# Down matrices of a SwiGLU layer: the running product read by ScalarE copies, and B22's casts placed between two of them

## The chip, the cores and the metric

One core of one Trainium2 chip. The metric is the device time of one execution in microseconds (us), the median of several runs. The engines of the core are TensorE (PE in the profile; PEld is its weight load), VectorE (DVE), ScalarE (ACT), GpSimd (POOL) and SyncE (SP), whose queue issues the DMA transfers (SPq).

## The reference

One layer of a streaming-encoder trunk on x of 1024 tokens by 1024 features, all in float32: RMSNorm, a combined input projection, three groups of heads (spatial gating, a conformer convolution, a gated delta rule), an output projection and a residual; then the part of this study, a SwiGLU feed-forward with D_FF = 2816 and its residual, and a final RMSNorm.

```python
x = x + jnp.einsum("bte,ed->btd", mix, w_out[l])
h = rms_norm(x, ffn_norm_g[l])
ff = jax.nn.silu(jnp.einsum("btd,df->btf", h, w_gate[l])) * jnp.einsum("btd,df->btf", h, w_up[l])
x = x + jnp.einsum("btf,fd->btd", ff, w_down[l])
return rms_norm(x, final_norm_g)
```

## The kernel before

Activations stand transposed: features on the 128 partitions, tokens on the free axis, in two halves of 512. To keep float32 accuracy, each operand is split into a high part (a cast to fp32r on ScalarE) and a low part (original minus high part, on VectorE), and each product is made in three passes: high by high, high by low, low by high. `split` and `split_w` (L127 to 132) do the splitting.

The feed-forward matrices are multiplied block-wise in 2 by 2 blocks with 7 products instead of 8. A `Matrix` stands for one such set of weights; its seven weight blocks are named w1 to w7 and meet the seven activation blocks B11 (w1), B21 (w2), T2 (w6), T1 (w5), T3 (w7), T4 (w4) and B22 (w3). One product (`product`, L799 to 803) is 12 matmuls of 128x128 by 128x512: four slices of the contraction by three passes. The products w1, w6, w7 and w4 run on in one PSUM tile X: after each, the value of X is read out before the next product adds to it. w2 goes to Y, w5 and w3 to Z. GpSimd forms the sums s1, s2 and s3 of the weight blocks (L836 to 838), from which w6, w5 and w7 are split, and then s2 again (L847) for w3; this last sum overwrites s2 and so waits for w6's low part.

The list `seq` holds 22 gate and up matrices, then 8 down matrices in two groups of four: d00, d02, d04, d06 and d10, d12, d14, d16 (group, first output tile). A group covers 8 of the 22 tiles of the feed-forward's features; the last six are multiplied after the down matrices, into the tiles pdl. Each down matrix takes the activation blocks of its group, which the gate and up matrices left in DRAM (FFd). `Group.load` and `Group.split` (L1044 to 1067) fetch and split them; B22 and T3 keep their halves in wider tiles, named B22B22f and T3hT3f/T3lT3f in the profile. The residual xad of one output tile and token half is loaded (`acc`), added to by `add` (L1005 to 1009), and stored again (`put`, L1003) after its last addition.

A gate or up matrix copies X to SBUF on ScalarE after w1, w6 and w7 (c11, c12 and c22: L828, L863, L868), and VectorE works on the copy. A down matrix instead reads X on VectorE: `add` takes X, Y or Z from PSUM and adds it to the residual, seven times per matrix (from X four times, from Y once, from Z twice). The next product into X cannot start before the addition that reads X is done.

The main loop (L1119 to 1172) writes the program in this order for each matrix: product6, product5, product7, then w1 and w2 of the next matrix (`first`) where that is not done yet, the splits of the next matrix's other weights (`rest`), and w4 and w3 (`end`). Ahead of a group, the first two products of its second and third matrix are done early (`early`), and then those of its first. The order of each engine's instructions is settled by a scheduler from this program when the kernel is built; engines run their rows in order and wait on one another by semaphores. In the kernel before, the group's splits of T3, T4 and B22 stand at the end of the step of the last matrix ahead of the group. Weights come in raw tiles of 512 KB (`load_raw`, L136, two buffers) and are released when their last block is split or summed.

## Time and profile before

| | us |
|---|---|
| median of 3 runs (1170.41 to 1175.22) | 1175.08 |
| profiled execution | 1176.49 |
| its span in the profile | 1174.5 |
| TensorE busy | 1139.2 (97%) |
| VectorE busy | 794.1 (68%) |
| ScalarE busy | 482.1 (41%) |
| GpSimd busy | 300.9 (26%) |
| mean granted clock of TensorE | 0.989 of full speed |

The span runs from the first to the last instruction that the profiler recorded; the execution's own time has some 2 us around it. The busy time of TensorE is modelled from pipelined matmuls: one is recorded at 0.39 to 0.40 us, while the next starts 0.23 us later. The down matrices lie between 914 and 1098 us of the span. The chain of work that ended last is 82% TensorE, 6% VectorE, 5% DMA, 3% issue, 2% GpSimd and 1% ScalarE.

### The profile page before, as it was taken

Reading aid. Unit: us, or ns where it says so; the run is one execution under the profiler, and the core shown is the slowest. Engines: PE = TensorE matmul, PEld = TensorE weight load, DVE = VectorE, ACT = ScalarE, POOL = GpSimd, SP = SyncE. Lnnn points to the kernel's source line nnn. Section 1 sums busy time; section 2 is a strip of 40 time slices with the busy share of each in tenths; the row PEclk is TensorE's granted clock in tenths of the full one; section 3 lists DMA queues with packets and bytes.
Section 4 is the critical chain, followed back from the end, with each engine's and each line's share of the span. In section 5 each row is a group of like instructions: output and inputs, shape, how many; then the busy total and the mean of one; then the engine's idle time right before and its main releaser. Section 6 shows DMA issues by size and latency. Waiting matters only on the chain.

```text
span 1174.5 us, 16043 instructions
## 1 busy us (share of the span) xinstructions
PE 1139.2 (97%) x5878; PEld 940.2 (80%) x5878; DVE 794.1 (68%) x1250; ACT 482.1 (41%) x1007; POOL 300.9 (26%) x234
## 2 busy tenths in 40 slices
PE   9999999999899999979999999999999979989997
PEld 7889888889688778858888888888888867868897
DVE  7699879868987666686555655565445767856523
ACT  6456561224235644354333333333334523423422
POOL 3000140010613221244323333333332232232142
PEclk9999999999999999999999999999999989999998
DMA  6235342463313455314222322232335778678212
GB/s 222 69 94 185 109 126 108 117 206 112 123 65 108 134 180 170 109 54 151 100 99 90 126 90 99 90 126 90 107 126 175 247 258 278 213 252 293 93 63 82
DMA packets 87182, 162.66 MB, mean 138 GB/s; under 512 B 16416, under 2 KB 28352, under 8 KB 87104
## 3 DMA queue, kind: packets, MB, share of 16 engines
q1 hardware_dynamic: 87104, 161.64, 41.4%
q8 instruction: 46, 0.75, 0.3%
q14 instruction: 32, 0.26, 0.1%
HBM read 114.93 MB, written 46.68 MB: 138 GB/s over the span
## 4 chain that ended last, share of the span: by engine, by line
PE 82%; DVE 6%; DMA 5%; issue 3%; POOL 2%; ACT 1%; SPq 0%; POOLq 0%; DVEq 0%; ACTq 0%
PE Xu L802 10%; PE Xg L802 10%; PE po L727 7%; PE pdl L1087 5%; PE Xd L802 5%; PE Zu L802 5%; PE Zg L802 5%; PE pv L228 4%; PE pq L228 4%; PE pk L228 3%; PE Yu L802 3%; PE pg L228 2%; PE Yg L802 2%; PE Zd L802 2%; DMA d_r<-in_wd_dram 2%
## 5 line engine op out<-in xcount | busy, mean ns | idle before, releaser
L664 DVE SCALAR_TENSOR_TENSOR ca<-cy,vec,ca 128x512 f32<-128x512 f32 x120 | 93.6, 801 | 0.5
L836 POOL TENSOR_TENSOR s1u<-u_r 128x512 f32<-128x512 f32 x11 | 23.6, 2149 | 81.3 <-DMA u_r<-in_wu_dram 81.3
L131 DVE TENSOR_TENSOR wo_l<-wo_r,wo_h 128x512 fp32r<-128x512 f32 x32 | 27.0, 854 | 24.3 <-ACT wo_h L130 24.2
L836 POOL TENSOR_TENSOR s1d<-d_r 128x512 f32<-128x512 f32 x8 | 10.7, 1334 | 110.8 <-DMA d_r<-in_wd_dram 110.8
L869 DVE TENSOR_TENSOR c22u<-Zu,c22u 128x512 f32<-128x512 f32 x11 | 7.6, 692 | 45.3 <-ACT c22u L868 45.3
L847 POOL TENSOR_TENSOR s2g<-g_r,s2g 128x512 f32<-128x512 f32 x11 | 19.0, 1727 | 71.5 <-DVE w6g_l L131 63.4
L789 POOL TENSOR_TENSOR sqa<-sqa,xr 128x512 f32<-128x512 f32 x13 | 18.0, 1384 | 71.8 <-ACT xr L787 44.1
L1007 DVE TENSOR_TENSOR xad<-Xd,xad 128x512 f32<-128x512 f32 x32 | 21.9, 686 | 20.7 <-PE Xd L802 20.6
L1241 POOL TENSOR_TENSOR sqf<-sqf,sqt 128x256 f32<-128x256 f32 (+1 forms) x19 | 17.9, 941 | 69.6 <-ACT sqt L1239 67.9
L847 POOL TENSOR_TENSOR s2u<-u_r,s2u 128x512 f32<-128x512 f32 x11 | 18.5, 1679 | 59.9 <-DVE w6u_l L131 59.9
L836 POOL TENSOR_TENSOR s1g<-g_r 128x512 f32<-128x512 f32 x11 | 15.0, 1368 | 66.6 <-DMA g_r<-in_wg_dram 66.6
L130 ACT CAST wo_h<-wo_r 128x512 fp32r<-128x512 f32 x32 | 19.6, 616 | 28.2 <-PE po L727 19.9
L1087 PE MATMUL pdl<-ff_h,wd_h 128*128 128x256 f32 (+1 forms) x96 | 30.9, 322 | 0.0
L1087 PE MATMUL pdl<-ff_h,wd_l 128*128 128x256 f32 (+1 forms) x96 | 30.5, 318 | 0.0
L1087 PE MATMUL pdl<-ff_l,wd_h 128*128 128x256 f32 (+1 forms) x96 | 30.5, 318 | 0.0
L1232 DVE TENSOR_TENSOR xf<-pdl,xf 128x256 f32<-128x256 f32 (+1 forms) x18 | 9.2, 514 | 28.3 <-PE pdl L1087 28.3
L802 PE MATMUL Xg<-b,w1g_h 128*128 128x512 f32 x88 | 27.6, 394 | 0.0
L802 PE MATMUL Yu<-b,w2u_h 128*128 128x512 f32 x88 | 27.6, 394 | 0.0
L802 PE MATMUL Xu<-b,w1u_h 128*128 128x512 f32 x88 | 27.6, 394 | 0.0
L802 PE MATMUL Yg<-b,w2g_h 128*128 128x512 f32 x88 | 27.5, 394 | 0.0
L868 ACT COPY c22g<-Xg 128x512 f32<-128x512 f32 x11 | 6.5, 587 | 48.3 <-PE Xg L802 48.3
L727 PE MATMUL po<-myc_l,wo_h 128*128 128x512 f32 x64 | 25.6, 400 | 0.7 <-DVE myc_l L90 0.7
(580 smaller groups left out, 3927.9 us busy)
## 6 DMA issues: line engine op xcount, KB each, us to landing
u_r<-in_wu_dram SPq DMA_DIRECT2D x24, 512.0 KB, 3.9
d_r<-in_wd_dram SPq DMA_DIRECT2D x24, 512.0 KB, 4.2
g_r<-in_wg_dram SPq DMA_DIRECT2D x23, 512.0 KB, 3.7
wo_r<-in_wout_dram SPq DMA_DIRECT2D x16, 512.0 KB, 3.8
xad<-X1d SPq DMA_DIRECT2D x32, 256.0 KB, 4.4
X1d<-xad SPq DMA_DIRECT2D x28, 256.0 KB, 3.2
FFd<-T SPq DMA_DIRECT2D x24, 256.0 KB, 2.0
xr<-in_xT_dram SPq DMA_DIRECT2D x16, 256.0 KB, 3.6
```

Source lines behind the costliest of these rows:

```text
L130: ACT.copy(hi, raw)
L131: DVE.tensor_tensor(lo, raw, f32(hi), op=ALU.subtract)
L228: proj.last = PE.matmul(ps[hf], lhsT=cols(wtile, a, kt * P), rhs=(xh, xl)[b][kt][hf], start=(kt == 0 and a + b == 0), stop=(kt == KT - 1 a ...
L664: DVE.scalar_tensor_tensor(o, y(m), w(m), o, op0=ALU.mult, op1=ALU.add)
L727: out_mm.last = PE.matmul(ps, lhsT=cols(wtile, a, kt * P), rhs=mix[hf][kt][b], start=(kt == 0 and a + b == 0), stop=(kt == 3 and a == 1))
L789: POOL.tensor_tensor(acc, acc, xr, op=ALU.add)
L802: PE.matmul(ps, lhsT=w[a][:, k * P:(k + 1) * P], rhs=blk[b][k], start=(first and k == 0 and a + b == 0), stop=(last and k == HB - 1 and a ...
L836: POOL.tensor_tensor(self.s1, a21, a22, op=ALU.add)
L847: (eng or POOL).tensor_tensor(self.s2, self.part(0, 1), self.s2, op=ALU.subtract)
L1007: DVE.tensor_tensor(x, ps, x, op=ALU.add)
L1087: PE.matmul(ps[:, 0:cs.stop - cs.start], lhsT=cols(wtile, a, c), rhs=ff[f, hf][b][:, cs], start=(first and i + a + b == 0), stop=(last and ...
L1241: POOL.tensor_tensor(acc[:, 0:w], acc[:, 0:w], t[:, 0:w], op=ALU.add)
```

## The change

The three methods of a down matrix that multiply into X now call those of `Matrix`. ScalarE copies X to c11, c12 or c22; VectorE adds Y to c11 and Z to c22, and then the copy to the residual. The number of VectorE operations per matrix stays at seven: of the four that read X and the three that read Y or Z, one from X and one from Z stay additions from PSUM into the residual, two read PSUM into c11 or c22, and three have both inputs in SBUF. ScalarE gets three copies of 128x512 per down matrix, 24 in all. The casts and subtractions that split B22 move from the end of the step before the group to behind product6 of the group's first matrix.

```diff
@@ -1002,32 +1002,28 @@
             if self is not seq[-1]:
                 nc.sync.dma_start(X1d[self.f[i], hf], self.x[i, hf])
 
-        def add(self, i, hf, ps, last=False):
+        def add(self, i, hf, t, last=False):
             x = self.x[i, hf]
-            DVE.tensor_tensor(x, ps, x, op=ALU.add)
+            DVE.tensor_tensor(x, t, x, op=ALU.add)
             if last:
                 self.put(i, hf)
 
         def begin(self, mid=None):
-            n, self.x = self.name, {}
-            self.X, Y = mm_ps(f"X{n}"), aux(f"Y{n}")
+            self.x = {}
             self.acc(0, 0)
-            product(self.X, self.w1, self.blk["B11"], True, False)
-            self.add(0, 0, self.X)
-            product(Y, self.w2, self.blk["B21"], True, True)
-            self.add(0, 0, Y, True)
+            super().begin(mid)
+            self.add(0, 0, self.c11, True)
 
         def product6(self):
             self.acc(0, 1)
-            product(self.X, self.w6, self.blk["T2"], False, False)
-            self.add(0, 1, self.X)
+            super().product6()
+            self.add(0, 1, self.c12)
 
         def product7(self):
             for i in range(2):
                 self.acc(1, 1 - i)
-            product(self.X, self.w7, self.blk["T3"], False, False)
-            self.add(1, 1, self.X)
-            self.add(1, 1, self.Z, True)
+            super().product7()
+            self.add(1, 1, self.c22, True)
 
         def end(self):
             product(self.X, self.w4, self.blk["T4"], False, True)
@@ -1127,6 +1123,8 @@
             last_tiles()
         if i > 0:
             m.product6()
+            if i in opener:
+                opener[i].split("B22")
             if new:
                 new.split("B11")
             m.product5()
@@ -1166,7 +1164,6 @@
             new.split("T3")
             new.load("B22")
             new.split("T4")
-            new.split("B22")
         if i >= FT and nxt is not None and i + 4 >= len(seq):
             for k in (0, 1) if i + 4 == len(seq) else (2, 3) if i + 3 == len(seq) else (4, 5):
                 load_late(LAST + k, 0)
```

The methods of `Matrix` that are now called stand unchanged:

```python
        def begin(self, mid=None):
            n = self.name
            self.X, Y = mm_ps(f"X{n}"), aux(f"Y{n}")
            product(self.X, self.w1, self.blk["B11"], True, False)
            if mid:
                mid()
            self.c11 = dt(f"c11{n}")
            ACT.copy(self.c11, self.X)
            product(Y, self.w2, self.blk["B21"], True, True)
            DVE.tensor_tensor(self.c11, Y, self.c11, op=ALU.add)
...
        def product6(self):
            product(self.X, self.w6, self.blk["T2"], False, False)
            self.c12 = dt(f"c12{self.name}")
            ACT.copy(self.c12, self.X)

        def product7(self):
            product(self.X, self.w7, self.blk["T3"], False, False)
            self.c22 = dt(f"c22{self.name}")
            ACT.copy(self.c22, self.X)
            DVE.tensor_tensor(self.c22, self.Z, self.c22, op=ALU.add)
```

How this moves instructions, at three places. The names carry the matrix (w6d00_l is the low part of w6 of d00) and a buffer number; c, X, Y and Z are the tiles above.

ScalarE at the first down matrix. Before, around the first cast of B22:

```order
L130 CAST w4d00_h_8261<-d001_r_8169 128x512
L130 CAST w3d00_h_8266<-s2d00_8244 128x512
L1066 CAST B22B22f000_8311<-B22B22f010_8313 128x512
L130 CAST w6d02_h_8396<-s2d02_8391 128x512
L130 CAST w5d02_h_8400<-s1d02_8390 128x512
L1066 CAST B22B22f000_8311<-B22B22f010_8313 128x512
L1066 CAST B22B22f001_8312<-B22B22f011_8314 128x512 x2
L130 CAST w7d02_h_8404<-s3d02_8392 128x512
```

Now:

```order
L1062 CAST T4f0h3_8328<-T4f0l3_8018 128x512
L863 COPY c12d00_8351<-Xd00_8185 128x512
L1062 CAST B22B22f000_8317<-B22B22f010_8319 128x512 x2
L1062 CAST B22B22f001_8318<-B22B22f011_8320 128x512 x2
L868 COPY c22d00_8391<-Xd00_8185 128x512
L130 CAST w6d02_h_8406<-s2d02_8401 128x512
```

The four casts stood among those of d02's weights, and now stand between the copies of c12 and c22 of d00. In the second group, one of the four stands ahead of c12 of d10 and three behind it.

TensorE at the end of w7 of d00. Before:

```order
L802 MATMUL Xd00_8179<-T3lT3f01_8238,w7d00_h_8257 128x512
L802 MATMUL Xd00_8179<-T3hT3f01_8235,w7d00_l_8258 128x512
L802 MATMUL Xd02_8093<-T2f0h0_8210,w6d02_h_8396 128x512
L802 MATMUL Xd02_8093<-T2f0l0_7704,w6d02_h_8396 128x512
L802 MATMUL Xd02_8093<-T2f0h0_8210,w6d02_l_8397 128x512
L802 MATMUL Xd02_8093<-T2f0h1_8213,w6d02_h_8396 128x512
L802 MATMUL Xd00_8179<-T4f0h0_8319,w4d00_h_8261 128x512
```

Now:

```order
L802 MATMUL Xd00_8185<-T3lT3f01_8244,w7d00_h_8263 128x512
L802 MATMUL Xd00_8185<-T3hT3f01_8241,w7d00_l_8264 128x512
L802 MATMUL Xd00_8185<-T4f0h0_8325,w4d00_h_8267 128x512
L802 MATMUL Xd00_8185<-T4f0l0_8015,w4d00_h_8267 128x512
L802 MATMUL Xd00_8185<-T4f0h0_8325,w4d00_l_8268 128x512
```

Four matmuls of the next matrix's w6 stood between w7 and w4 of one matrix; now w4 follows w7 at once.

VectorE ahead of w6's low part of d00. Before, from w2's low part on:

```order
L131 TENSOR_TENSOR w2d00_l_8176<-d001_r_8169,w2d00_h_8175 128x512
L1067 TENSOR_TENSOR T1f0l0_7712<-T1f0l0_7712,T1f0h0_8222 128x512
L1007 TENSOR_TENSOR xad0400_8138<-Yd04_8137,xad0400_8138 128x512
L1067 TENSOR_TENSOR T1f0l1_7713<-T1f0l1_7713,T1f0h1_8225 128x512
L1067 TENSOR_TENSOR T1f0l2_7714<-T1f0l2_7714,T1f0h2_8228 128x512
L1067 TENSOR_TENSOR T1f0l3_7715<-T1f0l3_7715,T1f0h3_8231 128x512
L131 TENSOR_TENSOR w6d00_l_8250<-s2d00_8244,w6d00_h_8249 128x512
```

Now the last twelve of the sixteen that run from w2's low part to w6's:

```order
L1063 TENSOR_TENSOR T2f0l1_7705<-T2f0l1_7705,T2f0h1_8219 128x512
L1063 TENSOR_TENSOR T2f0l2_7706<-T2f0l2_7706,T2f0h2_8222 128x512
L830 TENSOR_TENSOR c11d00_8199<-Yd00_8186,c11d00_8199 128x512
L1063 TENSOR_TENSOR T2f0l3_7707<-T2f0l3_7707,T2f0h3_8225 128x512
L1007 TENSOR_TENSOR xad0000_8183<-c11d00_8199,xad0000_8183 128x512
L1063 TENSOR_TENSOR T1f0l0_7712<-T1f0l0_7712,T1f0h0_8228 128x512
L1063 TENSOR_TENSOR T1f0l1_7713<-T1f0l1_7713,T1f0h1_8231 128x512
L1063 TENSOR_TENSOR T1f0l2_7714<-T1f0l2_7714,T1f0h2_8234 128x512
L1063 TENSOR_TENSOR T1f0l3_7715<-T1f0l3_7715,T1f0h3_8237 128x512
L971 TENSOR_TENSOR c21g10_8001<-Xu10_7915,c21g10_8001 128x512
L1063 TENSOR_TENSOR T3lT3f00_8243<-T3lT3f00_8243,T3hT3f01_8241 128x512
L131 TENSOR_TENSOR w6d00_l_8256<-s2d00_8250,w6d00_h_8255 128x512
```

All four subtractions of T2, which stood ahead of w2's low part before, and both additions of c11 of d00 now stand between the two low parts. (w2d00_l, the addition of Y to c11 of d04, that of c11 to d04's residual and the first T2 subtraction stand ahead of these rows.) In the second group the same holds: between w2's and w6's low part of d10 there was one subtraction of T4, and there are twelve operations now: eight subtractions of T2 and T1, the two of c11, and the last two additions of d06.

## Rows read from the trace of the kernel before

**Rows 1.** The page's busy times by engine: us, share of the span, instructions.
```profile
PE 1139.2 (97%) x5878; PEld 940.2 (80%) x5878; DVE 794.1 (68%) x1250; ACT 482.1 (41%) x1007; POOL 300.9 (26%) x234
```

**Rows 2.** TensorE's waits, 900 to 1110 us: line, waited for: us, times, longest us.
```profile
PE Xd L802 <- DVE xad L1007: 12.4, 3, 6.3
PE Xd L802 <- DVE w6d_l L131: 0.2, 1, 0.2
```

**Rows 3.** Stretches of 10 us: busy of PE, PEld, DVE, ACT, POOL; clock, DMA share, GB/s.
```profile
940.00:950.00 10.00, 3.72 (x14) 2.71 (x13) 10.00 (x12) 3.83 (x7) 6.16 (x4) 0.90 0.84 272
950.00:960.00 10.00, 10.00 (x35) 7.95 (x34) 5.77 (x10) 1.24 (x2) 0.00 (x0) 0.76 0.69 244
1030.00:1040.00 10.00, 5.56 (x18) 4.16 (x17) 5.74 (x8) 3.73 (x7) 5.43 (x4) 0.84 0.94 347
```

**Rows 4.** TensorE's timeline: start us, us, engine, line, operation, [idle before it, for what].
```profile
914.56 0.40 PE L802 MATMUL Xu<-T3h,w7u_l 128*128 128x512 f32 x1
...
937.05 0.39 PE L802 MATMUL Xd<-T2f0h,w6d_h 128*128 128x512 f32 x1
...
942.36 0.40 PE L802 MATMUL Zd<-T1f0h,w5d_l 128*128 128x512 f32 x1
...
949.04 0.77 PE L802 MATMUL Xd<-T3hT3f,w7d_h 128*128 128x512 f32 x1 [6.28 <-DVE xad L1007]
...
955.01 0.39 PE L802 MATMUL Xd<-T2f0h,w6d_l 128*128 128x512 f32 x1
...
972.23 0.50 PE L802 MATMUL Xd<-T4f0h,w4d_h 128*128 128x512 f32 x1 [1.68 <-DVE xad L1007]
...
1026.57 0.39 PE L802 MATMUL Xd<-T2f1h,w6d_h 128*128 128x512 f32 x1
...
1036.70 0.72 PE L802 MATMUL Xd<-T3hT3f,w7d_h 128*128 128x512 f32 x1 [4.44 <-DVE xad L1007]
...
1040.19 0.40 PE L802 MATMUL Xd<-T3hT3f,w7d_l 128*128 128x512 f32 x1
```

**Rows 5.** VectorE's timeline, same columns.
```profile
927.63 1.26 DVE L131 TENSOR_TENSOR w2d_l<-d_r,w2d_h 128x512 fp32r<-128x512 f32 x1 [1.46 <-ACT w2d_h L130]
...
928.82 1.78 DVE L1067 TENSOR_TENSOR T1f0l<-T1f0l,T1f0h 128x512 fp32r<-128x512 f32 x1
...
933.43 0.68 DVE L131 TENSOR_TENSOR w6d_l<-s2d,w6d_h 128x512 fp32r<-128x512 f32 x1
...
934.64 1.40 DVE L131 TENSOR_TENSOR w5d_l<-s1d,w5d_h 128x512 fp32r<-128x512 f32 x1
...
940.17 0.68 DVE L131 TENSOR_TENSOR w3d_l<-s2d,w3d_h 128x512 fp32r<-128x512 f32 x1
...
948.21 0.68 DVE L1007 TENSOR_TENSOR xad<-Xd,xad 128x512 f32<-128x512 f32 x1
...
948.81 1.37 DVE L1067 TENSOR_TENSOR B22B22f<-B22B22f,B22B22f 128x512 fp32r<-128x512 f32 x1
...
971.50 0.68 DVE L1007 TENSOR_TENSOR xad<-Xd,xad 128x512 f32<-128x512 f32 x1
...
1015.48 1.24 DVE L131 TENSOR_TENSOR w2d_l<-d_r,w2d_h 128x512 fp32r<-128x512 f32 x1 [1.54 <-ACT w2d_h L130]
```

**Rows 6.** ScalarE's timeline, same columns.
```profile
915.00 0.59 ACT L868 COPY c22u<-Xu 128x512 f32<-128x512 f32 x1 [1.17 <-PE Xu L802]
...
942.72 0.62 ACT L1066 CAST B22B22f<-B22B22f 128x512 fp32r<-128x512 f32 x1 [6.57 <-DMA B22B22f<-FFd]
```

**Rows 7.** GpSimd's timeline, same columns.
```profile
928.42 1.62 POOL L837 TENSOR_TENSOR s2d<-s1d,d_r 128x512 f32<-128x512 f32 x1
...
934.19 1.30 POOL L847 TENSOR_TENSOR s2d<-d_r,s2d 128x512 f32<-128x512 f32 x1 [2.44 <-DVE w6d_l L131]
```

**Rows 8.** VectorE's additions from Xd by tile: ns min/median/max, first and last start, form.
```profile
L1007 DVE TENSOR_TENSOR xad<-Xd,xad x32: 676/690/693, 918.9 to 1094.5; 128x512 f32<-128x512 f32 x32
```

**Rows 9.** Waits in SyncE's DMA queue, 880 to 1100 us: us, times, longest us.
```profile
SPq L1003 <- DVE xad L1007: 46.1, 26, 5.7
```

## The prediction

> **What bounds the kernel now.** First the busy times: TensorE is busy 1139.2 of the span's 1174.5 us, and no other engine comes near [rows 1]. So only TensorE's gaps and its slow stretches are to be had, and the change touches only the stage of the down matrices, from about 914 to 1098 us. Second, TensorE's waits in that stage: three, 12.4 us in all, are for a VectorE addition that reads Xd, and one of 0.2 us is for a low part [rows 2]. Third, the table by stretches: where the two long waits lie, the granted clock is 0.90 and 0.76 (940 to 960 us) and 0.84 (1030 to 1040 us), elsewhere 1.00 [rows 3].
>
> Fourth, TensorE's own rows show each wait [rows 4]. The first matmul of d00's w7 comes 6.28 us late, d02's w4 1.68 us, d10's w7 4.44 us. Full speed is one matmul every 0.231 us (937.05 to 942.36 is 23 steps). After the first wait, 14 matmuls take from 949.04 to 955.01, 5.97 us instead of 3.23; after the third, 8 take from 1036.70 to 1040.19, 3.49 instead of 1.85. These are 1.2 GHz stretches: 2.7 and 1.6 us lost. After 1.68 us of waiting the pace stayed.
>
> Why is the addition late? VectorE's rows say it [rows 5]: the addition of w6's product starts at 948.21, and the matmul that waits for it at 949.04. The product itself was done before w5's last matmul, at 942.36; the addition stood in VectorE's row behind subtractions and gate/up work that ran without a gap from 928.82.
>
> **The change, term by term** (against the profiled execution).
>
> *Removed.* With ScalarE reading X, none of the three waits needs VectorE: 12.4, with the 0.2 and the slow stretches 2.7 and 1.6: **16.9 us**. VectorE's count stays; ScalarE gets 24 copies. One takes 0.59 us; one such copy started at 915.00 where the last matmul into its tile began at 914.56 with a duration of 0.40 [rows 4, 6], so it is 0.04 us from product to copy. 24 x 0.59 = 14 us lie on an engine with 41% use [rows 1]; only where TensorE waits do they count. c12's copy, between w6 and w7, costs nothing: ten matmuls of w5 (2.3 us) stand there and cover 0.40 + 0.04 + 0.59; without that cover it would cost 0.85 as below.
>
> *c22 between w7 and w4.* In the changed row TensorE has w4 right behind w7 of the same matrix in d00, d02, d06, d10, d12 and d16; before, four to six matmuls of another product often stood between. (In d04 and d14 w1 and w2 of the next matrix cover the copy.) From the start of the last w7 matmul: 0.40 + 0.04 + 0.59, and 0.05 to the next matmul (the 1.68 us wait's addition ends at 971.50 + 0.68, and the matmul is at 972.23 [rows 4, 5]), less the step of 0.231: 0.85 us, six times: **5.1**. Low end 0.6 each, the copy alone (3.6); high end 1.68 each (10.1), the shortest of today's waits. 0.85 is built from rows of the same operation.
>
> *w6's low part of d00.* Fifteen operations now stand from behind w2's low part to w6's low part: additions of c11 and all T2 and T1 subtractions, some of which before filled VectorE's waits for loads. From 928.82 to 940.17 before also did fifteen in 11.35 us. One of these took 1.40 instead of 0.68 while GpSimd formed w3's sum, which in both kernels waits for w6's low part and so now runs behind it: 0.72 less, ready at 939.45, seen by TensorE at 939.50. TensorE wants it with its fifth matmul from 937.05, at 937.97: a wait of **1.5**. Low end 0 (fifteen at a plain step of 0.60, from 948.21 to the next start, 948.81: 937.8). High end 5.4: the pace of the six operations from 927.63 to 933.43, 0.97 (928.82 + 14.5 = 943.4) [rows 5, 7].
>
> What slows them: a subtraction started at 928.82 took 1.78; GpSimd's sum ran from 928.42 to 930.04 [rows 5, 7]. Additions that read PSUM took 676 to 693 ns, all 32 [rows 8]. With two inputs in SBUF the new additions belong to the slow kind. The Trainium skill (SBUF — State Buffer, section SBUF: two separate sides) says that a VectorE instruction with two SBUF inputs and a GpSimd instruction exclude each other for a whole instruction; the trace agrees (930.04 to 930.60 is 0.56, about one plain operation). By that rule each sum holds up one VectorE operation, whichever it is, and the wait stays 1.5; if each of the two new additions in the fifteen paid 1.78 - 0.60 on top, it would be 3.9.
>
> *w6's low part of d10.* Before, it stood two places behind w2's low part (1015.48); now thirteen, the last but one being the addition of d06's w3 product, whose last matmul starts one step before 1026.57 and ends at 1026.74. Addition and subtraction make 1028.1, wanted at 1027.49: 0.65 at least. But TensorE is then some 6 us ahead, and w2's low part, for which VectorE waited 1.54 us on the cast of a freshly loaded matrix, follows only as raw buffers come free. If it did not move up at all: 1015.48 + 1.24 + 12 x 0.757 (the pace of the fifteen) = 1025.8, the low part's 0.7 more, wanted at 1021.5: 5.0. I take **2.4**, with loads moving some 2.5 of the 6; the ends are 0.65 and 5.0 [rows 4, 5].
>
> *w6 of d02 and d04.* d02's low part now follows the additions of c22 and of w4's product; d04's waits for a load and sums that came just in time before. **1.0** together, ends 0 and 4.4 (today's third wait).
>
> *B22's casts.* Four in a row on ScalarE, now ahead of d00's c22 copy, in d10 one ahead of c12 and three ahead of c22. A cast takes 0.62, and in before ScalarE waited 6.57 us for the first to land, at 942.72 [rows 6]. c22 of d00 is wanted at 937.05 + 1.5 + 36 x 0.231 = 946.9, so the casts fit; in d10 c12 waits for one: **0.5** (ends 0 and 6.6, that whole wait).
>
> *Sum.* 5.1 + 1.5 + 2.4 + 1.0 + 0.5 = 10.5 given back of 16.9: **6.4 us faster**. 1176.49 - 6.4 = 1170.1; the profiled execution was 1.4 above the median of the three runs, so **1168.7**. All low ends: 3.6 + 0.65 = 4.3 back, 1162.5. A measurement here can tell about 0.5% (5.9 us) from no change.
>
> **Rivals.** *A: the waits only move.* Loads set the pace: d04's low part was late already in before (0.2 us, [rows 2]), and what TensorE gains early it waits for again at d04 (4.4) and d10 (5.0). Back: 5.1 + 1.5 + 5.0 + 4.4 + 0.5 = 16.5, 1174.7. Against it: SyncE issues the loads in order, behind stores that wait for the last additions of each matrix, and those come earlier with TensorE (46.1 us in 26 such waits [rows 9]).
>
> *B: only the copies cost.* If low parts and loads keep up, 5.1 + 0.65: 11.1 faster, 1164.0. For it: VectorE has slack beyond 951 us (5.77 busy of 10 at 950 to 960 [rows 3]).
>
> *C: VectorE falls behind, slower.* The place is the fifteen before w6's low part of d00 and the twelve in d10. All of these but the few with Y or X read two SBUF inputs. At 0.95 us each d00 waits 5.1 and the slow clock comes back (2.7): 6.3 more than my sum, no change. From about 1.15 it is slower by over 0.5%; at 1.2, the price of w2's low part beside GpSimd (1.26, 1.24 [rows 5]), d00's low part comes at 946.8 (8.9 late, 7.4 more than in my sum, and 2.7); d10's, if loads are late with the rest, 1015.48 + 1.24 + 12 x 1.2 + 1.2 = 1032.3 against 1027.49: 4.8, 2.4 more, and 1.6. Together 14.1 more, 1182.8. Against it: GpSimd's sums fill only part of the stretch.
>
> *D: c22 is stuck behind B22.* If B22 lands 6 us later than before, the casts end at 942.72 + 6 + 4 x 0.62 = 951.2 instead of being done by 946.9: 4.3 us, and 1.6 of slow clock after it as after the third wait: 1174.6. *That the change does not do what it says* is out: in the changed row every such matmul waits for ScalarE's copy.
>
> **How the numbers follow.** Forecast 0.50 (its own range 1164.5 to 1172.5; two thirds of it, 0.33, is over 0.5% faster, 0.17 within), A 0.17, B 0.14, C 0.13, D 0.06. Faster 0.33 + 0.14 = 0.47; same 0.17 + 0.17 + 0.06 = 0.40; slower 0.13. The range runs from the low ends, 1162.5, to 1178, past A and D and short of C's 1182.8.
>
> **What would show it.** Right: no wait of Xd for a VectorE addition; six waits for c22 of about 0.85; waits for w6's low part of 1.5 (d00) and 2.4 (d10); granted clock near 1.00 in the stretches of [rows 3]; 24 copies at 0.59; additions of c up to 1.78 beside GpSimd. Wrong: waits for low parts above 5 us or a clock under 0.95 again (C), waits for loads or GpSimd's sums (A), a c22 wait of several us behind a cast (D).

## The result, and the profile after

The changed kernel takes 1179.51 us (median of 8 runs, 1177.63 to 1185.01), the kernel before 1173.51 (8 runs, 1170.41 to 1175.22). The ratio is 1.0057, with a 95% interval of 1.0043 to 1.0072: **slower by 0.57%**. The forecast was 1168.7, its range 1162.5 to 1178.

Executions of one kernel differ: one of the change lies 5.5 us above its median, and a profile shows only one execution. So the runs below are compared by ratios, and profiles, with that reserve, by the length of one **stage**: from the first matmul of the last w4 of an up matrix to the first matmul of pdl with wdl. It is 174.0 us in the profile before and 177.3 in that of the change.

TensorE's waits in the changed kernel, from 880 to 1110 us (columns as in [rows 2]):

```profile
PE Xd L802 <- ACT c22d L868: 4.0, 6, 0.7
PE Xd L802 <- ACT c12d L863: 3.1, 2, 1.8
PE Xd L802 <- ACT w6d_h L130: 2.6, 1, 2.6
PE Xd L802 <- DVE w6d_l L131: 2.5, 2, 1.7
PE Yd L802 <- DVE w2d_l L131: 1.0, 1, 1.0
PE pdl L1083 <- ACT wd_h L130: 1.0, 1, 1.0
```

Not one wait for an addition on VectorE is left of the 12.4 us of [rows 2]. In its place stand six kinds of wait, 14.2 us together. The first was foreseen, six times. Waits for w6's low part were foreseen too, and those of this profile are shorter (0.80 and 1.71 us, for 1.5 and 2.4). The others are new or larger than foreseen.

The stretches of the changed kernel, columns as in [rows 3]:

```profile
940.00:950.00 10.00, 8.06 (x34) 5.96 (x33) 8.16 (x15) 5.86 (x11) 2.04 (x2) 1.00 0.76 274
950.00:960.00 10.00, 9.96 (x43) 7.75 (x43) 7.46 (x9) 3.50 (x6) 5.67 (x4) 1.00 0.51 173
...
970.00:980.00 10.00, 8.03 (x28) 6.09 (x29) 6.48 (x8) 4.21 (x8) 4.28 (x4) 0.83 0.48 145
1030.00:1040.00 10.00, 8.21 (x29) 5.99 (x27) 8.02 (x14) 5.26 (x10) 2.85 (x2) 0.83 0.72 249
```

From 940 to 960 us the granted clock is back at 1.00 (0.90 and 0.76 in [rows 3]). But it falls to 0.83 at 970 to 980 us, where it was full before, and at 1030 to 1040 it is as low as in [rows 3].

TensorE's timeline, columns as in [rows 4]:

```profile
938.46 0.50 PE L802 MATMUL Xd<-T2f0h,w6d_l 128*128 128x512 f32 x1 [0.80 <-DVE w6d_l L131]
...
944.63 0.50 PE L802 MATMUL Xd<-T3hT3f,w7d_h 128*128 128x512 f32 x1 [1.27 <-ACT c12d L863]
...
948.34 0.50 PE L802 MATMUL Xd<-T4f0h,w4d_h 128*128 128x512 f32 x1 [0.68 <-ACT c22d L868]
...
971.97 0.79 PE L802 MATMUL Xd<-T2f0h,w6d_h 128*128 128x512 f32 x1 [2.62 <-ACT w6d_h L130]
...
975.33 0.39 PE L802 MATMUL Xd<-T2f0l,w6d_h 128*128 128x512 f32 x1
...
1028.96 0.50 PE L802 MATMUL Xd<-T2f1h,w6d_l 128*128 128x512 f32 x1 [1.71 <-DVE w6d_l L131]
...
1035.65 0.50 PE L802 MATMUL Xd<-T3hT3f,w7d_h 128*128 128x512 f32 x1 [1.79 <-ACT c12d L863]
```

w7 of d00, 6.28 us late in [rows 4], is 1.27 late, and w7 of d10 1.79 instead of 4.44. In d04, whose w6 was 0.2 late, w6 now waits 2.62 us for its high part, and its next seven steps take 3.36 us (971.97 to 975.33) instead of 1.62: 1.7 us lost in a stretch whose granted clock is 0.83, that is, partly at 1.2 GHz.

Two chains lie behind these waits. **The first is c12's copy in d00.** ScalarE's timeline, columns as in [rows 6]:

```profile
941.39 0.62 ACT L130 CAST w3d_h<-s2d 128x512 fp32r<-128x512 f32 x1 [3.39 <-POOL s2d L847]
941.92 2.18 ACT L1062 CAST T4f0h<-T4f0l 128x512 fp32r<-128x512 f32 x4
944.00 0.57 ACT L863 COPY c12d<-Xd 128x512 f32<-128x512 f32 x1
```

The product that c12 copies was done soon after its last matmul began at 940.62, but the copy starts at 944.00. It stands in ScalarE's row behind four casts of T4, these behind w3's cast, and that one waits 3.39 us for a sum of GpSimd. GpSimd's and VectorE's timelines show why the sum is late:

```profile
938.48 2.88 POOL L847 TENSOR_TENSOR s2d<-d_r,s2d 128x512 f32<-128x512 f32 x1 [7.84 <-DVE w6d_l L131]
...
968.65 1.28 POOL L836 TENSOR_TENSOR s1d<-d_r 128x512 f32<-128x512 f32 x1 [12.27 <-DMA d_r<-in_wd_dram]
```

```profile
937.72 0.68 DVE L131 TENSOR_TENSOR w6d_l<-s2d,w6d_h 128x512 fp32r<-128x512 f32 x1
938.32 0.68 DVE L131 TENSOR_TENSOR w5d_l<-s1d,w5d_h 128x512 fp32r<-128x512 f32 x1
938.92 0.68 DVE L131 TENSOR_TENSOR w7d_l<-s3d,w7d_h 128x512 fp32r<-128x512 f32 x1
939.53 0.68 DVE L131 TENSOR_TENSOR w4d_l<-d_r,w4d_h 128x512 fp32r<-128x512 f32 x1
```

The sum overwrites s2 and so waits for w6's low part, which now ends the long row of subtractions, at 938.4. Then it takes 2.88 us instead of the 1.30 of [rows 7].

**The second is d04's weights.** GpSimd's second row above waits 12.27 us for their load, until 968.65; w6's high part follows the sums at 971.29. SyncE's queue says why the load is late; first its waits, then its timeline (start, us, queue, line, transfer):

```profile
SPq L1003 <- DVE xad L1007: 65.0, 27, 6.0
SPq L1003 <- DMA xad<-X1d: 16.3, 6, 4.5
```

```profile
945.90 0.43 SPq L1054 DMA_DIRECT2D T2f1l<-FFd  x1
951.69 0.92 SPq L1003 DMA_DIRECT2D X1d<-xad  x2
952.66 1.43 SPq L1054 DMA_DIRECT2D T2f1l<-FFd  x3
954.13 0.43 SPq L1054 DMA_DIRECT2D T1f1l<-FFd  x1
958.75 0.32 SPq L1003 DMA_DIRECT2D X1d<-xad  x1
...
962.04 0.85 SPq L136 DMA_DIRECT2D d_r<-in_wd_dram  x2
```

The queue issues in its row's order. Two stores of the residual (L1003) hold it from 946.3 to 951.7 and one from 954.6 to 958.8, each waiting for an addition; behind them stand the loads of T2 and T1 and, last, at 962.04, the two of d04. The stores' waits for additions have grown from 46.1 us to 65.0 [rows 9]. Another 16.3 us, of a kind that the kernel before does not have, are put down to loads of the residual that an addition needs first.

In the kernel before, the same two loads are issued earlier, although its TensorE is behind at this point (w4 of d02 starts at 972.23 [rows 4], in the change at 963.51). SyncE's timeline there:

```profile
959.16 0.32 SPq L1003 DMA_DIRECT2D X1d<-xad  x1
959.58 0.88 SPq L136 DMA_DIRECT2D d_r<-in_wd_dram  x2
961.94 0.33 SPq L1003 DMA_DIRECT2D X1d<-xad  x1
```

They stand behind two of d00's last three stores, and the third comes after them. In the change all three stand ahead. The third waits for the addition of w3's product of d00. VectorE's timelines show it, first of the kernel before, then of the change:

```profile
961.22 0.69 DVE L1007 TENSOR_TENSOR xad<-Zd,xad 128x512 f32<-128x512 f32 x1 [1.49 <-PE Zd L802]
```

```profile
958.05 0.68 DVE L1007 TENSOR_TENSOR xad<-Zd,xad 128x512 f32<-128x512 f32 x1
```

Before, this addition starts when its product is done. In the change the product is done some 7 us earlier, soon after 954, but the addition comes only 3.2 us earlier, since it stands behind the five low parts of d02's weights (953.49 to 958.05).

What the additions themselves cost was as foreseen (by tile: ns min/median/max, as in [rows 8]):

```profile
L1007 DVE TENSOR_TENSOR xad<-c11d,xad x8: 677/682/1746, 922.7 to 1077.7; 128x512 f32<-128x512 f32 x8
...
L1007 DVE TENSOR_TENSOR xad<-c22d,xad x8: 685/692/1281, 950.6 to 1091.4; 128x512 f32<-128x512 f32 x8
```

### The profile page after: what moved, and what is told of

The parts are those of the page before. It is cut to its first block, busy times and chain, and to the rows that moved or that the text cites. A ratio compares the mean times of both kernels' runs of the same rounds, so it can differ in the third digit from the quotient of the medians.

```text
span 1176.9 us, 16026 instructions
## 1 busy us (share of the span) xinstructions
PE 1139.0 (97%) x5878; PEld 935.6 (79%) x5878; DVE 792.7 (67%) x1250; ACT 494.1 (42%) x1031; POOL 305.7 (26%) x234
## 4 chain that ended last, share of the span: by engine, by line
PE 83%; DVE 6%; DMA 4%; POOL 3%; issue 2%; ACT 1%; SPq 1%; POOLq 0%; DVEq 0%; ACTq 0%
PE Xu L802 10%; PE Xg L802 10%; PE po L727 7%; PE Xd L802 5%; PE pdl L1083 5%; PE Zu L802 5%; PE Zg L802 5%; PE pv L228 4%; PE pq L228 4%; PE pk L228 3%; PE Yu L802 3%; PE pg L228 2%; PE Yg L802 2%; PE Zd L802 2%; PE pu L306 2%
## 5 line engine op out<-in xcount | busy, mean ns | idle before, releaser
L868 ACT COPY c22u<-Xu 128x512 f32<-128x512 f32 x11 | 6.5, 587 | 45.8 <-PE Xu L802 45.8
```

## The experiments

Ratios are to the kernel before on the same chip, with 95% intervals.

### The kernel before once more, and its parts

> The kernel before, unchanged, for a second profile: the first one took 1176.5, 2.9 over the median of all runs, and the prediction's 16.9 us of removable loss were read from it. If the loss differs between executions (theory V), this one shows a sum of losses in the down stage other than 17.5, with the long waits behind w6 shorter or without the slow clock; if not, 17.5 within 1 us and the time near 1176.

One more execution of the kernel before took 1174.4 us. The same three waits are there, at the same places. The two long ones are shorter (4.2 and 3.6 us instead of 6.3 and 4.4), and the stage takes 170.8 us, not 174.0:

```profile
PE Xd L802 <- DVE xad L1007: 9.5, 3, 4.2
```

So the execution of [rows 2 to 4] had some 3 us more in just these waits than this one.

Then the parts. Each kernel is the one before with one or two of the three methods changed; the move of B22's casts was not run by itself, since put into the kernel before it leaves the row of every engine as it was.

```diff
 c11_only:  begin      self.x = {}; self.acc(0, 0)
+                      super().begin(mid)
+                      self.add(0, 0, self.c11, True)
 c12_only:  product6
+                      super().product6()
+                      self.add(0, 1, self.c12)
 c22_only:  product7
+                      super().product7()
+                      self.add(1, 1, self.c22, True)
 c12c22:    product6 and product7, both as above
```

> Only the c11 copies of the change (w1's product read by ScalarE, then Y added on VectorE); w6 and w7 are read by VectorE as before, B22 where it was. Theory S (the c11 copies pull the casts of T2, T1 and T4 behind them, and with them w6's low part and the first reader of w6's product, in d00 and d10): all the loss and none of the gain, w6's low part late by about 1 to 2 us in both groups and the waits for the addition behind w6 as long as before or longer: about 1180, at least 4 us over before. Rival L (SyncE's row decides: stores that wait for late additions hold up the loads of d04): the put of c11 comes no later than that of Y before, so no more than 2 us from before, about 1174. Rival B (B22's casts between the copies): no casts have moved, so as before, 1173.5.

> Only w6's product is read by a ScalarE copy; w1 and w7 by VectorE as before; T2, T1 and T4 casts stand as before, four to seven matmuls of the next matrix stand between w7 and w4 as before. Theory S: nearly the whole of the 16.9 us comes free and little is given back (c12's copy behind two casts of B22 in d00, about 1.5): 8 to 13 us faster, 1161 to 1166. Rival L: TensorE comes earlier but d04's weights don't, about 4.5 us with the slow clock after it: 1167 to 1170. Rival B: c12's copy stands between B22's casts and waits for them, 3 us or more in each group: about 1171.

> Only w7's product is read by a ScalarE copy. w4 stands right behind w7 in six matrices. Theory S: six waits of 0.68 with 0.17 for the copy's tail make 5.0; d02's wait of 1.7 goes; d00's and d10's long waits for the addition behind w6 stay: about 1176 to 1178. Rival L: the store of d00 comes later (c22 and its additions on VectorE), d04's loads late by 2 to 4 us more: about 1180. Rival B: as S, B22 stays in its place.

> Copies for c12 and c22, w1's product read by VectorE as before. Theory S: as c12_only with six waits of 0.85 more: 1166 to 1171, faster than before. Rival L: as the change itself at d04, so 1171 to 1174. Rival B: waits of several us for c22 behind B22's casts in both groups, above 1174.

| | median us | ratio | stage us | stores' wait for additions, us |
|---|---|---|---|---|
| c11_only | 1190.38 | 1.0155 (1.0122 to 1.0189) | 189.0 | 73.2 |
| c12_only | 1174.01 | 1.0005 (0.9989 to 1.0021) | 171.4 | 59.3 |
| c22_only | 1190.21 | 1.0138 (1.0116 to 1.016) | 185.3 | 82.4 |
| c12c22 | 1173.05 | 0.9989 (0.9973 to 1.0005) | 169.3 | 56.9 |
| the change | 1179.51 | 1.0057 (1.0043 to 1.0072) | 177.3 | 65.0 |

(The profile of c12c22 is of its fastest execution, 3.7 us under its median, so its stage reads short.)

The parts don't add up, and three of the four missed what was expected: c11_only and c22_only came out some 10 us above it, c12_only above all three theories. c11 alone and c22 alone each cost over 1%, and with them the waits for additions from X grew. TensorE's waits, first of c11_only, then of c22_only:

```profile
PE Xd L802 <- DVE xad L1007: 18.7, 7, 6.7
```

```profile
PE Xd L802 <- DVE xad L1007: 17.3, 5, 8.5
PE Xd L802 <- ACT c22d L868: 3.6, 6, 0.7
```

In both, eight subtractions of T4 and B22 stand in VectorE's row right ahead of an addition that reads Xd: from 942.44 to the addition at 947.25 in c11_only, from 1038.44 to the one at 1046.47 in c22_only. The last column is SyncE's queue: the two kernels with the longest stages are also those whose stores wait longest. c12 and c22 together change nothing that can be told. The change differs from c12c22 by c11 and by the place of B22's casts, and c12c22_ordered below has these casts between the two copies of d00, as in the change, and is no slower. So c11 on top makes the slowdown. In c12_only a copy meets the fate that the prediction gave to B22's casts; ScalarE's timeline at d10:

```profile
1030.78 1.22 ACT L1066 CAST B22B22f<-B22B22f 128x512 fp32r<-128x512 f32 x2 [8.83 <-DMA B22B22f<-FFd]
1031.90 0.58 ACT L863 COPY c12d<-Xd 128x512 f32<-128x512 f32 x1
```

The casts wait 8.83 us for their load, the copy behind them, and TensorE 5.1 us for the copy. Written by the program's order alone, a copy may end up behind casts.

### The copies ahead of the casts

Two kernels hold the casts back until c12's copy is issued: c12c22_ordered the casts of B22, on c12c22; after_t4_behind those of T4 and B22, on the change.

```diff
-            ACT.copy(self.c12, self.X)
+            self.c12_copy = ACT.copy(self.c12, self.X)
...
             if i in opener:
+                with tc.issue_after(m.c12_copy.ins):
+                    opener[i].split("T4")
+                    opener[i].split("B22")
```

> Copies for c12 and c22 only, and B22's casts forced behind c12's copy (in c12c22 two of them stood ahead of it and waited for B22's load). Theory T: c12's waits in d00 and d10 (1.05 and its tail, twice; 5.1 with slow clock in c12_only) go: 2 to 5 us under c12c22, 1168 to 1171, faster than before. Rival L: no gain, 1173.

> The change with one thing more: T4's casts too are made behind c12's copy of each group's first matrix, so that copy stands right behind w3's cast, no longer behind four T4 casts (and one of B22 in d10). Theory T (the copies that free X are late since they queue behind casts on ScalarE): the waits of w7 for c12 in d00 (1.3) and d10 (1.8) go, and the slow clock after the second (2.3): 3 to 6 us under the change, about 1175. Rival L (d04's load): unchanged, within 2 us of the change, 1178 to 1181. Rival C (VectorE's lateness with w6's low part sets everything): unchanged too, the time moves to c22 behind eight casts.

c12c22_ordered takes 1172.53, ratio 0.9988 (0.9971 to 1.0005), as c12c22; the gain expected by theory T did not come. Its waits for c12 are gone, but those for c22 are 8.0 us instead of 4.0, the longest 3.2: the casts now stand ahead of that copy. after_t4_behind takes 1181.5, 1.007 (1.0043 to 1.0096), as the change. In it TensorE no longer waits for c12, as wanted:

```profile
PE Xd L802 <- DVE w6d_l L131: 3.4, 3, 2.8
PE Xd L802 <- ACT w6d_h L130: 3.2, 1, 3.2
```

But w6's high part of d04 comes 3.2 us late instead of 2.6, w6's low part in d10 2.8 instead of 1.7: what TensorE gains ahead of d04 it waits for there. The late copy is real, but taking it away alone gains nothing.

c12c22_ordered also shows what c11 adds. By the measure of the last table of this document, its stage loses 15.7 us and that of the change 21.8. Of the difference, 1.1 us lie in d00, 1.7 in d02 and d04, 2.7 in d10 and 0.6 at the end. In c12c22_ordered, too, d04's loads stand behind d00's last three stores (they are issued from 960.99), and w6's high part of d04 is 2.1 us late. So most of d04's wait comes with the copies of c12 and c22, and c11's loss is spread over the stage.

### T2 and T1 at another time

c11's copies put the casts and subtractions of T2 and T1 behind them. t2t1_later loads the blocks one matrix later (and so takes these loads from ahead of d04's weights); after_t2t1_ahead splits T2 and T1 of the first group ahead of `first`.

```diff
 t2t1_later
-        new, coming = opener.get(i + 1), opener.get(i + 3)
+        new, coming = opener.get(i + 1), opener.get(i + 2)
 after_t2t1_ahead
+                if new.gi == 0:
+                    new.split("T2")
+                    new.split("T1")
...
-            new.split("T2")
-            new.split("T1")
+            if new.gi > 0:
+                new.split("T2")
+                new.split("T1")
```

> The change with the second group's T2 and T1 loads (eight, in SyncE's row ahead of d04's weights) one step later, so that d04's weights are issued behind two stores instead of behind eight loads, six residual loads and three stores. Rival L: d04's wait of 2.6 and the slow clock after it (1.7) go: 4 us under the change, about 1175. Theory T: the rows on ScalarE are as they were in d00, so d00 and d10 lose the same; if d04's wait stays, within 1.5 us of the change.

> The change, with T2's and T1's casts of the first group written ahead of d00's first product: on ScalarE they stand ahead of c11's copy of d00, and on VectorE w6's low part of d00 is two places behind w2's, as before. Theory T (c11's copies pull the casts back): the first group's waits of w6 (0.8) and of c12 (1.3) go or shrink to half, about 2 to 3 us come free in d00, and 2 us or more stay to the end: about 1177. Rival L: what d00 gains is lost at d04, where w6 starts at the same time as in the change (972): no gain, 1178 to 1181.

t2t1_later takes 1178.19, 1.0043 (1.0022 to 1.0063), not the 1175 expected if d04's load decided: d04's wait is gone, but w6 of d10 waits 3.1 us for its cast instead. after_t2t1_ahead takes 1179.14, 1.0048 (1.0032 to 1.0064): d00 has no wait for c12 nor for w6 any more, but w2 ahead of it waits 1.4 and 2.2 us, d04 2.9 and d10 2.8. Neither pays: the waits move.

### The stores of the residual: left out, or on GpSimd's queue

The kernels without stores leave out that part of the computation: a tile is loaded as if nothing had been added to it.

```diff
 before_no_put, after_no_put
         def put(self, i, hf):
-            if self is not seq[-1]:
-                nc.sync.dma_start(X1d[self.f[i], hf], self.x[i, hf])
+            pass
 before_put_pool, after_put_pool, split5_put_pool
-                nc.sync.dma_start(X1d[self.f[i], hf], self.x[i, hf])
+                nc.gpsimd.dma_start(X1d[self.f[i], hf], self.x[i, hf])
```

> The change without those 28 stores (the same left out). Rival L: what the change loses at d04 (4.5 with the slow clock) and ahead of d10 comes from loads behind stores; without stores it gains 8 us or more and comes out below before_no_put. Theory T: it gains as little as before_no_put does, and stays some 6 us over it.

> The kernel before without the 28 stores of the residual between matrices (left out: later matrices add to the old residual). Control for the next run. Rival L (SyncE's row and the transfers pace the stage): loads no longer stand behind stores that wait for additions, and 7 MB fewer are moved: the long waits behind w6 are VectorE's and remain, so 2 to 6 us under before. Theory T (queues on ScalarE and VectorE): within 2 us of before.

> The change with the 28 stores of the residual issued from GpSimd's row; all transfers stay. Place (theory L): d04's weights are issued some 4 us earlier, d04's wait and its slow clock (4.5) go: 5 to 8 us under the change, 1172 to 1175. Traffic: within 2 us of the change, 1178 to 1181. Against either: GpSimd's sums now wait behind stores that wait for additions.

> Control: the kernel before with its stores on GpSimd's row. Place: the loads of before were little held up, 0 to 2 us faster than before, 1172 to 1174. Traffic: the same as before. If it is slower than before, GpSimd's sums pay for the stores, and the price is to be added to that of after_put_pool.

| | median us | ratio | stage us |
|---|---|---|---|
| before_no_put | 1172.27 | 0.9977 (0.9963 to 0.9991) | 167.9 |
| after_no_put | 1172.73 | 0.9991 (0.9978 to 1.0005) | 170.4 |
| before_put_pool | 1176.55 | 1.0026 (1.0011 to 1.0041) | 176.1 |
| after_put_pool | 1177.04 | 1.0034 (1.0016 to 1.0053) | 174.4 |

Without stores the two kernels take the same within their intervals: by the ratios the stores cost the change 0.66% (1.0057 to 0.9991) and the kernel before 0.23%. That left two readings, the stores' place in SyncE's row or their traffic. (A third remains in all of these runs: the scheduler orders every kernel anew, and without stores, or with stores elsewhere, it also orders the rows of TensorE, VectorE and ScalarE differently.) GpSimd's queue does not decide between them, since the blocking moved along. GpSimd's timeline of after_put_pool at d04's weights:

```profile
968.28 0.54 POOL L1003 DMA_DIRECT2D X1d<-xad  x1 [5.71 <-DVE xad L1007]
968.83 1.31 POOL L836 TENSOR_TENSOR s1d<-d_r 128x512 f32<-128x512 f32 x1
```

Now the sum of the weights itself stands behind a store that waits 5.71 us for an addition, and starts no earlier than in the change (968.65).

### The stores behind the next matrix's loads

The next test keeps each store on SyncE and changes, in the program, its place alone.

```diff
+    late = []
+    def stores(keep=0):
+        while len(late) > keep:
+            nc.sync.dma_start(*late.pop(0))
...
-                nc.sync.dma_start(X1d[self.f[i], hf], self.x[i, hf])
+                late.append((X1d[self.f[i], hf], self.x[i, hf]))
...
+            stores()
```

`stores()` stands in the main loop behind `rest` of the next matrix, and ahead of the last tiles.

> The change with every store of the residual still issued on SyncE, but collected and issued after the loads of the next matrix instead of between its turns' loads. In SyncE's row the two loads of d04 then stand behind one waiting store instead of three; as many bytes are moved by the same queue. If the place of the stores in the row delays d04 (my theory): the wait for w6's high part in d04 (2.62 us and some 1.7 at the lower clock) is gone, the stage comes to about 171 to 174 us against 177.3 of the change, and the time to 1173 to 1176. If it is the traffic of the stores, which this kernel keeps and the kernel without stores did not: no gain, 1178 to 1181, stage about 177. The copies behind the casts (c12d's wait of d10) stay in both theories.

It takes 1171.28 us, ratio 0.9982 (0.9966 to 0.9997): 8.2 us under the change, more than expected, with the same bytes on the same queue. Its profile is of an execution of 1176.31, 5.0 us over the median, with a stage of 173.2, so it shows only part of the gain. The stores wait for additions as long as in the change (62.8 us against 65.0), but two of d00's last three no longer hold up d04's loads. SyncE's timeline there:

```profile
953.46 1.85 SPq L1060 DMA_DIRECT2D T1f1l<-FFd  x4
...
956.84 2.40 SPq L136 DMA_DIRECT2D d_r<-in_wd_dram  x2
959.28 7.34 SPq L991 DMA_DIRECT2D X1d<-xad  x3
```

d04's loads are issued from 956.84, not from 962.04, and the stores wait behind them; GpSimd's sums of d04 start at 965.66 instead of 968.65, and w6 of d04 waits for nothing. So d04's wait is traced to the place of the stores, and the number of bytes is excluded as its cause. Not all of the 8.2 us is shown to come from it. The scheduler ordered other rows anew here as well: in d10 the last two additions of d06 (1028.57 and 1029.17) stand behind w6's low part, no longer ahead of it as in the change (1027.04 and 1027.64), and that low part is 0.45 us late instead of 1.71. A kernel with these rows and the stores where they were was not run. Eight kinds of wait are left, 11.6 us, with the copies' own time and a longer chain at d10 as the largest (TensorE's waits):

```profile
PE Xd L802 <- ACT c22d L868: 3.4, 5, 0.7
PE Zd L802 <- DVE c22d L869: 2.6, 1, 2.6
PE Xd L802 <- ACT c12d L863: 2.1, 2, 1.3
```

The same place for the stores in the kernel before was not tried, so whether the change is worth anything with them there stays open; leaving the stores out gained the kernel before 0.23%.

### A version that beats both

split5 takes away the copies' own time: on c12c22_ordered it puts half of w5 between w7 and w4, so that matmuls into Z cover c22's copy.

```diff
         def product5(self):
+            self.Z = aux(f"Z{self.name}")
+            product(self.Z, self.w5, self.blk["T1"], True, False, range(2))
         def product7(self):
+            product(self.X, self.w7, self.blk["T3"], False, False)
+            self.c22 = dt(f"c22{self.name}")
+            ACT.copy(self.c22, self.X)
+            product(self.Z, self.w5, self.blk["T1"], False, False, range(2, HB))
+            DVE.tensor_tensor(self.c22, self.Z, self.c22, op=ALU.add)
```

split5_t2t1 adds the later load of T2 and T1, split5_put_pool the stores on GpSimd's queue, split5_put_late those behind the loads.

> c12c22_ordered with product w5 cut in two: half of it stands between w6 and w7 and half between w7 and w4, so that six matmuls (1.39 us) cover each copy. My sum: six waits of 0.85 go, 5.0 us, less what loads take back at d04: 2 to 5 us under c12c22_ordered, 1167.5 to 1170.5, and faster than before by 3 to 6. Rival L: all of it is taken back at d04 and d10, 1172 to 1173.

> split5 with the second group's T2 and T1 loads one step later. In the change this took away d04's wait and put one of 3.1 at d10 in its place, 1.3 us net. Expected: d04's wait goes here too and half or more comes back at d10: 0 to 3 us under split5, 1167 to 1170.5.

> split5 with the stores on GpSimd's row. In split5's profile d04 still waits 2.7 with 2.8 of slow clock after it, and d10's w1 and w2 some 4. Place: most of these go, 3 to 7 us under split5: 1163.5 to 1167. Traffic: as split5, 1169 to 1171.

> The fastest kernel so far with stores on SyncE (w5 split in two around w7, 1170.28) with the same move of the stores behind the next matrix's loads. By the place of the stores: 1166 to 1170, stage about 166 to 170. By their traffic: 1170 to 1172, stage about 171. It should stay below both kernels in either case.

| | median us | ratio | stage us |
|---|---|---|---|
| split5 | 1170.28 | 0.9969 (0.9953 to 0.9984) | 171.2 |
| split5_t2t1 | 1175.58 | 1.0013 (0.9998 to 1.0027) | 172.6 |
| split5_put_pool | 1167.82 | 0.9954 (0.9935 to 0.9974) | 165.0 |
| split5_put_late | 1173.24 | 0.9995 (0.9977 to 1.0013) | 174.2 |

split5 beats both kernels by a little; with the stores on GpSimd's queue it comes to 1167.82, the lowest of all, though the intervals of the two overlap. In split5 one wait of 0.9 us for c22 is left instead of six of 0.7. The later load of T2 and T1 makes it slower, against what was expected (1167 to 1170.5). The late stores don't help it either, a second miss: ScalarE's timeline at d10 shows c22's copy behind B22's casts, and these behind their load:

```profile
1034.33 2.58 ACT L1079 CAST B22B22f<-B22B22f 128x512 fp32r<-128x512 f32 x4 [5.74 <-DMA B22B22f<-FFd]
1036.82 0.58 ACT L1036 COPY c22d<-Xd 128x512 f32<-128x512 f32 x1
```

TensorE waits 3.9 us for this copy, and at d04 3.3 us for c12's. The wait at d10 is rival D's mechanism, in a kernel that runs ahead of its loads. Why B22 comes late there was not followed further.

## Why the prediction was wrong

Its terms against the profile of the change. A product's loss is the time from its first matmul to the next product's, less 0.2315 us for each of its matmuls.

| step of the prediction | said, us | measured, us |
|---|---|---|
| removed: three waits and the slow clock | 16.9 | 17.6 in that execution, 14.4 in the second |
| c22 between w7 and w4, six times | 5.1 | 5.2 |
| w6's low part of d00 | 1.5 | 1.0 |
| low parts of d10 (w2 and w6) | 2.4 | 3.2 |
| w6 of d02 and d04 | 1.0 | 4.8, of it 1.7 of slow clock |
| c12's copy (0) and B22's casts (0.5) | 0.5 | 5.0, of it 1.6 of slow clock |
| end of the stage (not named) | 0 | 1.2 |
| given back | 10.5 | 20.4 |

- **What was right.** No wait for an addition from Xd is left; the copies cost some 0.85 us each, six times; d00's low part and d10's were sized within 1 us; the additions' median is 0.68 to 0.69 us, and at most 1.75, so rival C, the one that ended slower, has its premise false.
- **"w6 of d02 and d04: 1.0."** This step measured 4.8, and its high end of 4.4 was too low as well. The argument against rival A was that the stores wait for additions "and those come earlier with TensorE". They do come earlier (the last of d00 at 958.05, before at 961.22), but d04's loads do not: they are issued at 962.04, before at 959.58, since in the change's row they stand behind all of d00's last three stores and not behind two, and since the third store's addition came only 3.2 us earlier where its product was some 7 us earlier. The stores' waits for additions grew by 18.9 us [rows 9]. after_put_late shows that with the loads ahead of two of the stores d04's wait is gone. It does not show that this step alone decides: t2t1_later took d04's wait away too, and gained little.
- **"c12's copy costs nothing: ten matmuls of w5 cover it."** The cover is there, but the price was taken for a copy that starts when its product is done. ScalarE's row had the copy behind w3's cast and T4's casts: 1.46 and 1.95 us lost, and 1.6 at the lower clock after the second. Measured against what was said, this term, put at 0.5 with B22's casts, is the one that is off most. The order of ScalarE's row showed the last of T4's casts right ahead of the copy; the prediction read only B22's from it. after_t4_behind shows, though, that taking this wait away alone was worth nothing.
- **"Removed: 16.9."** The slow stretches were gone where the waits were, but the clock fell again behind the two longest of the new waits (0.83 at 970 and at 1030 us). And the size came from one execution that was 3.0 us above the median of all eight runs; a second showed waits of 9.5 us. The forecast allowed 1.4.
- **The rivals.** By its mechanism the outcome is nearest to A (1174.7): what TensorE gains early it waits for again, at d04 for loads. A's sum lacked the copies behind casts, so it ended below what came. The time lies between A's and C's 1182.8, but C's mechanism, slow additions, is not there.

Given back less removed is 2.8 us by this table; the stage grew by 3.3. The runs settle this much: on top of c12 and c22, which change nothing that can be told, c11 makes the loss; and without the stores the change takes no longer than the kernel before without them. That the stores' place carries all of the loss is argued, not shown, since the other rows moved in those runs too. How much of c11's effect comes through VectorE's row and how much through GpSimd's longer sum was not separated.

## What to carry to other kernels

When a copy takes the place of a wait, its price is not its duration but its place in its engine's row: read what stands ahead of it there, and what that waits for. An in-order queue that holds both stores of results and loads of operands turns a delay of the results into a delay of the operands behind them; try the loads ahead of the stores that wait longest (8.2 us less on the change, nothing on split5), and look in its row first for what is late next. Where a scheduler orders the rows, a small edit moves rows on every engine: compare them before a gain is put down to the edit. Take the size of a wait from two executions before it is counted as a gain.

## What the runs showed of the hardware

GpSimd's sum of 128x512 took 2.88 us in the change, from 938.48 to 941.36, instead of 1.30 [rows 7]. VectorE ran the low parts of w5, w7 and w4 at 938.32, 938.92 and 939.53, each with two inputs in SBUF, and the step between them, 0.60 us, was that of undisturbed ones. 941.36 less 1.30 is 940.06, about the end of the last of the three (940.21). So the sum seems to have waited for the whole row of them, not for one, and VectorE lost nothing. In d10 it is the same: 2.88 us, from 1028.98.

The Trainium skill (SBUF — State Buffer, section SBUF: two separate sides) says that of a VectorE instruction with two inputs in SBUF and a GpSimd instruction that reads SBUF, the one that starts first keeps the other out until it is done. The trace agrees that they exclude each other; that the sum then comes behind two more of VectorE's is this trace's, in place of the one operation per sum that the prediction worked with.

The other side shows in c22_only: there four subtractions of T4 took 5.70 us, from 1038.44 on, instead of 2.49, while three sums ran from 1037.82 to 1043.0:

```profile
1038.44 5.70 DVE L1066 TENSOR_TENSOR T4f1l<-T4f1l,T4f1h 128x512 fp32r<-128x512 f32 x4
```
